# A planned decoder step on one Trainium2 core: eight complex powers move from GpSimd to VectorE, two TensorE steps get a later planned start, and the planner learns of a shared port

## The chip, the cores and the metric

The kernel runs on one core of one Trainium2 chip. The metric is the time of one execution on the device in microseconds (us). The engines are named as in the profile: PE is TensorE (PEld its weight loads), DVE is VectorE, ACT is ScalarE, POOL is GpSimd, and SP (SyncE) issues every DMA.

## The reference

One layer of a hybrid decoder over 2048 prompt tokens and 8 single sample tokens, model width 1024, everything in float32:

```python
h = rmsnorm(x, norm_mix_g)
z = h @ w_in                        # q, k, v | conv a, g | ssm u
attn_out = attend(q, k, v, sinks)   # 8 heads, window 128, ALiBi, sinks
conv_out = conv_module(...)         # GLU, depthwise conv of 31 taps, layer norm, silu
ssm_out  = ssm_module(...)          # 16 groups, 64 complex states, gelu, GLU
x = x + concat(attn_out, conv_out, ssm_out) @ w_out
hf = rmsnorm(x, norm_ffn_g)
x = x + (silu(hf @ w_ff_gate) * (hf @ w_ff_up)) @ w_ff_down
```

A final rmsnorm and the new caches and states are also outputs. Each sample token has a cache of 30 convolution rows, so its convolution needs `cache_conv` beside the new row. In the ssm the matrix that takes 8 tokens at once into a state holds the product of the input matrix with the powers 0 to 7 of each state's complex multiplier.

## The kernel before

**Tiling.** The tokens are cut in four quarters q of 512 columns (the last has 520, with the 8 sample tokens) for everything up to the output projection, and in three groups of 688 and 684 columns for the feed-forward part. A matrix product is made of three float32r products per term (high by high, high by low, low by high), so each weight unit of 128 output rows (a tile `whl`) takes 24 matmuls per column tile. Such a unit is prepared once: SP loads `wraw`, ACT writes the high part, POOL writes the low part (a subtraction, `yield low` in `load_unit`, line 349), and the result is also stored to memory, from where later quarters load it again.

**The first phase** (to about 600 us) runs the projections in the order of line 1280: convolution and ssm inputs of quarter 0, attention inputs of quarter 1, then of quarter 0, and so on to the convolution inputs of quarter 3 (`3c`). Beside it DVE sets up the ssm tables in `setup_ssm` (line 750): a chain of some 200 small instructions, which ends with the discretized input matrix `bb`; then `power(t)` (line 890) makes for each of 8 powers six instructions of 128x128 (four products, a difference, a sum) into the tiles `wr` and `wi`. PE transposes `wr` and `wi` once all eight are done (`yield pw_ev`, line 910). `setup_toeplitz` (line 931) makes, from the same `bb`, nine further steps of six DVE instructions into `GT`, which PE needs too. The convolution (`conv`, line 593) is 60 DVE instructions per quarter on a tile `acc`, followed by `layer_norm_gate` (line 609), which goes from POOL to PE to DVE to ACT and back. `conv_tail` (line 654) does the convolution of the sample tokens: it loads `cache_conv` into `crow`, transposes it on PE, and ends in another `layer_norm_gate` of 8 columns.

**The second phase** (to about 800 us) is the output projection, `out_stream` (line 1624), which adds the residual on DVE, squares on ACT, and sums the squares over the 8 output units on POOL into `ssq`; after the last unit (line 1668) PE multiplies `ssq` by the tile `ones_c`, ACT takes the root and DVE the reciprocal. **The rest** is the feed-forward part.

**What sets the order.** Every engine runs its instructions in the order in which they were issued, and that order is found by a planner while the program is built: class `Flow`. Each piece of work is a generator which yields the engine, the buffers and the events that it needs next. `Flow.run` keeps one planned clock per engine, takes the piece that can start earliest (by priority among those within a small slack), and lets it issue its instructions. `Engine.cost` gives each instruction a planned duration, and `Flow.spent` (line 139) moves the clock of its engine on by that. `Flow.freer` (line 132) picks the engine whose planned clock is behind, with 500 ns in favour of POOL; `power` uses it to choose between POOL and DVE. An `Ev` is an event with a planned time, before which a piece that yields it isn't planned. In the planner of before no engine's clock knows of another's port:

```python
start = max(self.clock[eng], c["begin"] if c["last"] in (None, eng) else c["fin"])
self.clock[eng] = start + ns
```

The planned times only set the order. What an instruction waits for when it runs are the semaphores of the data that it reads and of the buffers that it writes.

Of the kernel before, what the change touches and what calls it, by code (L numbers as in the profile page):

```python
# [13 lines left out]
OP = mybir.AluOpType  # L14
PSUM = bass.MemoryType.PSUM
# [12 lines left out]
NEG = -1.0e30  # L28
W = [512, 512, 512, 520]
TILES = [[(0, 512)]] * 3 + [[(0, 256), (256, 264)]]  # L30
C1 = 6.28125
C2 = 0.0019350051879882812
C3 = 3.0199159819567e-07
# [17 lines left out]
class Flow:  # L51
# [9 lines left out]
    def __init__(self, nc):  # L61
        self.nc = nc
        self.clock = dict.fromkeys(("PE", "ACT", "DVE", "POOL", "SP", "DMA"), 0.0)
        self.free = {}
        self.tasks = []
        self.cur = None
        self.serial = 0
        self.extra = {}

    def buffers(self, **tags):  # L70
        for tag, n in tags.items():
# [57 lines left out]
    def now(self):  # L129
        return self.cur["fin"]  # L130

    def freer(self, *engines):
        return min(engines, key=lambda x: self.clock[x] + self.BIAS.get(x, 0.0))

# [1 line left out]
        self.free[tag].append(self.cur["fin"])  # L136
        self.free[tag].sort()

    def spent(self, eng, ns):
        c = self.cur  # L140
        if c is None:
            return
        ns += self.extra.get(eng, 0.0)
        start = max(self.clock[eng], c["begin"] if c["last"] in (None, eng) else c["fin"])
        self.clock[eng] = start + ns
        c["fin"], c["last"] = max(c["fin"], start + ns + self.LATENCY[eng]), eng
        c["end"], c["prev"] = start + ns, eng
# [15 lines left out]
class Engine:  # L163
# [36 lines left out]
    def __getattr__(self, op):  # L200
        call = getattr(self.engine, op)

        def planned(*args, **kw):
            out = args[0] if args else kw["out"]
            ins = [x for x in args[1:] if isinstance(x, bass.AP)]
            ins += [x for k, x in kw.items() if isinstance(x, bass.AP) and k not in ("out", "accum_out")]
            self.flow.spent(self.name, self.cost(op, out, ins, args, kw))
            return call(*args, **kw)  # L208
        return planned

# [2 lines left out]
def hybrid_step(  # L213
# [10 lines left out]
    fl = Flow(nc)  # L224
# [63 lines left out]
    def stg():  # L288
        return stage.tile([P, 520], F32, tag="stg", name="stg", bufs=N_ST)
# [364 lines left out]
    def conv_tail():  # L654

        yield "SP", "stg", "stg", small_ev, cu_ev[3, 0], cu_ev[3, 1], halo_ev[3]
        cu = CU[3]
        crow = stg()
        for a in range(2):
            dma(crow[:120, a * 256:(a + 1) * 256], cache_conv[0, 4 * a:4 * a + 4].rearrange("b t c -> (b t) c"))  # L660
        cs = stg()[:, 0:2 * NS * TAPS].rearrange("p (i b t) -> p i b t", i=2, b=NS)
        for i in range(2):
            yield "PE", "tr"
            pt = ps_tr()
            for a in range(2):
                E.transpose(pt[:, a * 120:a * 120 + 120], crow[:120, a * 256 + i * P:a * 256 + (i + 1) * P],
                            ident[:120, :120])
            yield "DVE"
            V.tensor_copy(cs[:, i, :, 0:30], pt[:, 0:240].rearrange("p (b t) -> p b t", t=30))
            V.tensor_copy(cs[:, i, :, 30], cu[:, i, 542:550])  # L670
            rel("tr")
        yield "PE", "tr"
        po = ps_tr()
        for i in range(2):
            E.transpose(po[:38, i * P:(i + 1) * P], cu[:, i, 512:550], ident)
        yield "DVE"
        V.tensor_copy(crow[:38, 0:256], po[:38, 0:256])
        rel("tr")
        cu_done(3)
        yield "SP"  # L680
        dma(o_convp[0, 0], crow[:30, 0:256])
        dma(o_convs[0, :, 29, :], crow[30:38, 0:256])
        rel("stg")
        yield "DVE"
        acc = cpool.tile([P, 2, NS], F32, name="acc_s")
        for i in range(2):
            V.tensor_tensor(cs[:, i], cs[:, i], taps[:, i:i + 1, :].to_broadcast([P, NS, TAPS]), op=OP.mult)
            V.tensor_reduce(out=acc[:, i, 0:NS], in_=cs[:, i], op=OP.add, axis=mybir.AxisListType.X)
            V.tensor_scalar(acc[:, i, 0:NS], acc[:, i, 0:NS], fv[:, i:i + 1], None, op0=OP.add)
        rel("stg")  # L690
        fl.add(layer_norm_gate(acc, NS, 3, 512), 2.5)
# [58 lines left out]
    def setup_ssm():  # L750
# [124 lines left out]
        ta, tb = tv(0, 8, 16), tv(1, 8, 16)  # L875
# [12 lines left out]
        pw_ev = Ev(8)  # L888

        def power(t):  # L890
            eng = fl.freer("POOL", "DVE")
            yield eng
            X = G if eng == "POOL" else V
            ta, tb = [tp[:, (2 * (t % 2) + i) * P:(2 * (t % 2) + i + 1) * P].rearrange("p (s c) -> p s c", c=16)
                      for i in range(2)]
            pr, pi = bc16(PW[:, 0, 7 - t, :]), bc16(PW[:, 1, 7 - t, :])
            dr, di = [w.rearrange("p (s t c) -> p s t c", t=8, c=16)[:, :, t, :] for w in (wr, wi)]
            X.tensor_tensor(dr, bb3[0], pr, op=OP.mult)
            X.tensor_tensor(ta, bb3[1], pi, op=OP.mult)
            X.tensor_tensor(di, bb3[0], pi, op=OP.mult)  # L900
            yield eng
            X.tensor_tensor(tb, bb3[1], pr, op=OP.mult)
            X.tensor_tensor(dr, dr, ta, op=OP.subtract)
            X.tensor_tensor(di, di, tb, op=OP.add)
            pw_ev.hit(fl.now())
            if t < 6:
                fl.add(power(t + 2), -900)
# [716 lines left out]
    def out_stream():  # L1624
        for q in range(4):
            yield "stg", Mev[q]
            ssq = stg()
            chain = Ev()
            chain.hit(0.0)
            boxes = []  # L1630
            for m in range(KT):
                ev, box = Ev(), []
                boxes.append((ev, box))
            fl.add(residual(q, 0, *boxes[0]), -600)
            for m in range(KT):
                if m + 1 < KT:
                    fl.add(residual(q, m + 1, *boxes[m + 1]), -400)
                st = {"n": nt[q], "chain": chain}
                chain = Ev()

                def evac(ps, c0, n, q=q, m=m, ev=boxes[m][0], box=boxes[m][1], st=st, ssq=ssq, nxt=chain):
                    yield "DVE", ev
                    x2 = box[0]
                    V.tensor_tensor(x2[:, c0:c0 + n], ps[:, :n], x2[:, c0:c0 + n], op=OP.add)
                    rel("mm")
                    st["n"] -= 1
                    if st["n"]:
                        return
                    yield "SP"
                    dma(x2_d[m][:, 512 * q:512 * q + W[q]], x2[:, :W[q]])  # L1650
                    x2_ev[q, m].hit(fl.now())
                    w = W[q]
                    if m == 0:
                        yield "ACT", st["chain"]
                        S.activation(ssq[:, :w], x2[:, :w], AF.Square)
                        rel("x2")
                        segB_ev.hit(fl.now())
                    else:
                        yield "ACT", "stg"
                        sq = stg()  # L1660
                        S.activation(sq[:, :w], x2[:, :w], AF.Square)
                        rel("x2")
                        segB_ev.hit(fl.now())
                        yield "POOL", st["chain"]
                        G.tensor_tensor(ssq[:, :w], ssq[:, :w], sq[:, :w], op=OP.add)
                        rel("stg")
                    nxt.hit(fl.now())
                    if m == KT - 1:
                        yield "stg"
                        rs = stg()  # L1670
                        for c0, n in TILES[q]:
                            yield "PE", "tr"
                            pm = ps_tr()
                            E.matmul(pm[:, :n], ones_c, ssq[:, c0:c0 + n], start=True, stop=True)
                            yield "ACT"
                            S.activation(rs[:, c0:c0 + n], pm[:, :n], AF.Sqrt, scale=256.0 / D, bias=eps)
                            rel("tr")
                        rel("stg")
                        yield "DVE"
                        V.reciprocal(rs[:, :w], rs[:, :w])  # L1680
                        yield "SP"
                        dma(rs_d[:, 512 * q:512 * q + w], rs[:, :w])
                        rel("stg")
                        rs_ev[q].hit(fl.now())
                yield from dense(outs[KT * q + m], M[q], TILES[q], evac, -500)
            rel("h")

# [366 lines left out]
    b = "B22"  # L2054
# [180 lines left out]
```

## Time and profile before

| | us |
|---|---|
| three runs | 2240.51, 2243.15, 2245.12 (median 2243.15) |
| the profiled execution, its own time | 2244.29 |
| its span, from the first to the last instruction | 2242.5 |

So 1.8 us of the profiled execution's time lie outside its span, and it is 1.1 us above the median. The profile's page gives the busy time of each engine and the chain that ended last. Its timelines list an engine's instructions in order of time, neighbours of one kind merged, with the idle time ahead in brackets and whose result ended it. All matrix work has the line L208 (the planner's helper), so instructions are told apart by the tiles that they write and read: `mm` and `sc` are accumulators of products, `tr` the accumulators for transposes and small products, `s` the tiles of the ssm and of attention, `PW` the powers.

### The profile page before, as it was taken

What the parts mean: (1) busy time and instruction counts of PE and PEld (TensorE: products, weight loads), DVE (VectorE), ACT (ScalarE), POOL (GpSimd) and SP (SyncE); (2) the same over time, 40 slices, a digit from 0 to 9 for tenths busy, and PEclk for the clock granted to TensorE, in tenths of its full rate; (3) what the DMA queues carried; (4) which work ended last, traced back from release to release, by engine and by line L of the source; (5) the groups of instructions that cost most, each with busy time, mean ns of one, the idle gap of its engine ahead of it and who ended that gap; (6) DMA issues with size and microseconds to landing.
All of it is one profiled execution on the core that took longest, in us unless ns stands there. A gap on an engine that the chain in (4) does not pass through costs nothing. (4 is left out here: it accounts for less than half of the span.)

```text
span 2242.5 us, 35196 instructions
## 1 busy us (share of the span) xinstructions
PE 2110.6 (94%) x13326; PEld 1961.5 (87%) x13326; DVE 1554.2 (69%) x3039; ACT 834.9 (37%) x1653; POOL 281.1 (13%) x219
## 2 busy tenths in 40 slices
PE   8779998999889989999999999999999999999997
PEld 8557776777667878999999999999999999999997
DVE  5986988786595567878877765656556755555555
ACT  7116534776333143323323452322223532222223
POOL 3421011002212232222222100000000000000000
PEclk9889999999989999999999999999999999999999
DMA  8856566566769996555664766575665774553651
GB/s 275 250 185 217 180 201 195 157 190 197 250 220 312 332 305 211 199 166 196 196 210 158 250 228 220 181 228 158 190 215 170 235 255 140 180 184 126 191 162 51
DMA packets 350713, 457.90 MB, mean 204 GB/s; under 512 B 42453, under 2 KB 233760, under 8 KB 340304
## 3 DMA queue, kind: packets, MB, share of 16 engines
q1 hardware_dynamic: 350544, 455.66, 63.7%
q8 instruction: 105, 1.72, 0.3%
q14 instruction: 64, 0.52, 0.1%
HBM read 333.94 MB, written 122.32 MB: 203 GB/s over the span
## 5 line engine op out<-in xcount | busy, mean ns | idle before, releaser
L208 PE MATMUL mm<-h,whl 128*128 128x342 f32 (+4 forms) x7296 | 1277.3, 331 | 37.7 <-POOL whl L208 13.9
L208 PEld LDWEIGHTS mm<-h,whl 128*128 128x128 f32 x7296 | 1156.4, 191 | 106.1 <-issue 20.4
L208 PE MATMUL sc<-act,whx 128*128 128x342 f32 (+1 forms) x3168 | 517.6, 321 | 8.3 <-DVE xa L208 6.4
L208 PEld LDWEIGHTS sc<-act,whx 128*128 128x128 f32 x3168 | 501.3, 189 | 12.5 <-DVE xa L208 10.6
L208 DVE TENSOR_TENSOR xa<-xa,sc 128x342 f32<-128x342 f32 (+1 forms) x528 | 266.0, 510 | 235.5 <-PE sc L208 226.6
L208 DVE SCALAR_TENSOR_TENSOR acc<-cu,taps,acc 128x512 f32<-128x512 f32 x240 | 174.6, 791 | 0.1
L208 POOL TENSOR_TENSOR whl<-sw,whl 128x512 fp32r<-128x512 f32 x88 | 124.6, 1427 | 344.6 <-ACT whl L208 337.5
L208 ACT ACTIVATE whx<-wraw 128x1024 fp32r<-128x1024 f32 x66 | 66.6, 1053 | 240.3 <-PE sc L208 238.8
L208 ACT ACTIVATE stg<-mm 128x342 f32<-128x342 f32 (+3 forms) x100 | 49.5, 499 | 252.0 <-PE mm L208 249.8
L208 PE MATMUL mm<-hb,whl 128*128 128x342 f32 (+1 forms) x792 | 135.8, 320 | 0.0
L208 PEld LDWEIGHTS mm<-hb,whl 128*128 128x128 f32 x792 | 126.5, 189 | 0.4 <-ACT gs L208 0.4
L208 ACT ACTIVATE whl<-wraw 128x512 fp32r<-128x512 f32 (+1 forms) x122 | 84.7, 696 | 68.5 <-PE mm L208 28.2
L208 DVE TENSOR_TENSOR stg<-mm,stg 128x342 f32<-128x342 f32 (+1 forms) x132 | 67.7, 513 | 57.2 <-PE mm L208 55.0
L208 ACT ACTIVATE act<-gs 128x342 fp32r<-128x342 f32 (+1 forms) x99 | 48.3, 488 | 145.4 <-DVE gs L208 145.4
L208 DVE TENSOR_TENSOR whl<-wraw,whl 128x512 fp32r<-128x512 f32 x102 | 78.1, 766 | 30.9 <-ACT whl L208 28.7
L208 ACT ACTIVATE s<-s,sst 128x256 f32<-128x256 f32 (+1 forms) x180 | 83.4, 486 | 10.9 <-DVE sst L208 10.8
L208 ACT ACT_TABLE_LOAD x58 | 74.4, 1283 | 30.4 <-DVE acc L208 10.9
L208 DVE TENSOR_TENSOR whl<-xraw,whl 128x512 fp32r<-128x512 f32 x96 | 76.5, 802 | 11.1 <-ACT whl L208 11.1
L208 DVE TENSOR_TENSOR whx<-wraw,whx 128x1024 fp32r<-128x1024 f32 x66 | 79.0, 1236 | 5.5 <-ACT whx L208 2.2
L208 ACT ACTIVATE whl<-sw 128x512 fp32r<-128x512 f32 x88 | 53.1, 625 | 75.9 <-PE mm L208 28.2
L208 ACT ACTIVATE whl<-xraw 128x512 fp32r<-128x512 f32 x96 | 60.0, 625 | 49.0 <-issue 29.7
L208 DVE TENSOR_TENSOR gs<-mm,gs 128x342 f32<-128x342 f32 (+1 forms) x66 | 33.7, 511 | 59.9 <-PE mm L208 59.9
(233 smaller groups left out, 1890.6 us busy)
## 6 DMA issues: line engine op xcount, KB each, us to landing
whl<-sum SPq DMA_DIRECT2D x176, 512.0 KB
sum<-whl SPq DMA_DIRECT2D x88, 512.0 KB
wraw<-in_w_ff_down SPq DMA_DIRECT2D x66, 512.0 KB
whl<-hl_o SPq DMA_DIRECT2D x24, 1024.0 KB
wraw<-in_w_ff_up SPq DMA_DIRECT2D x44, 512.0 KB
xraw<-in_w_ff_gate SPq DMA_DIRECT2D x42, 512.0 KB
whl<-hl_q SPq DMA_DIRECT2D x12, 1024.0 KB
tx<-hraw SPq DMA_DIRECT2D x14, 684.0 KB
```

The costliest lines, as they stand in the source:

```text
L208: return call(*args, **kw)
```

## The change

It has four edits. `power` no longer asks which engine is behind: all of its instructions go to DVE. `conv_tail` adds an event 6 us after its load of `cache_conv`, so that the planner puts the transposes of `crow` no earlier. In `out_stream` the product with `ones_c` gets an event 8 us after the last sum of squares. And the planner keeps a list of the times at which POOL, and DVE instructions with two operands of more than one column outside PSUM, hold a port in common: an instruction of the one isn't planned to start inside a time of the other.

```diff
+RS_LATE = 8000.0
...
+    def later(self, ns):
+        ev = Ev()
+        ev.hit(self.cur["fin"] + ns)
+        return ev
...
-    def spent(self, eng, ns):
+    def spent(self, eng, ns, port=False):
...
         start = max(self.clock[eng], c["begin"] if c["last"] in (None, eng) else c["fin"])
+        if port:
+
+            for a, b in self.port["POOL" if eng == "DVE" else "DVE"]:
+                if a <= start < b:
+                    start = b
+            self.port[eng] = self.port[eng][-40:] + [(start, start + ns)]
         self.clock[eng] = start + ns
...
-            self.flow.spent(self.name, self.cost(op, out, ins, args, kw))
+            both = self.name == "DVE" and sum(x.space != PSUM and x.free_size() > 1 for x in ins) > 1
+            self.flow.spent(self.name, self.cost(op, out, ins, args, kw), self.name == "POOL" or both)
...
         cs = stg()[:, 0:2 * NS * TAPS].rearrange("p (i b t) -> p i b t", i=2, b=NS)
+        ready = fl.later(6000.0)
         for i in range(2):
-            yield "PE", "tr"
+            yield "PE", "tr", ready
...
         def power(t):
-            eng = fl.freer("POOL", "DVE")
-            yield eng
-            X = G if eng == "POOL" else V
+            yield "DVE"
...
-            X.tensor_tensor(dr, bb3[0], pr, op=OP.mult)
+            V.tensor_tensor(dr, bb3[0], pr, op=OP.mult)
...
                     if m == KT - 1:
-                        yield "stg"
+                        yield "stg", fl.later(RS_LATE)
```

The order of all engines moves with the planned times, from about 20 us on. From the middle of the first group of the feed-forward part to the end the kinds of the instructions follow each other as before on PE, DVE and ACT. Three places show what moved. The numbers behind a name tell tiles of one kind apart and differ between the kernels.

On POOL, at the end of the preparation of the first 12 weight units (`whl<-wraw,whl`), before. Here `s2_1085` holds `bb`, `s4_1103` and `s4_1104` are `wr` and `wi`, and `s2_1105` is the tile for temporary products:

```order
L208 TENSOR_TENSOR whl_1026<-wraw_918,whl_1026 128x1024
L208 TENSOR_TENSOR s4_1103<-s2_1085,PW_168 128x8x16
L208 TENSOR_TENSOR s2_1105<-s2_1085,PW_168 128x128
L208 TENSOR_TENSOR s4_1104<-s2_1085,PW_168 128x8x16
L208 TENSOR_TENSOR whl_1093<-wraw_998,whl_1093 128x1024
L208 TENSOR_TENSOR s2_1105<-s2_1085,PW_168 128x128
```

And now (`whl_1046` is the unit that was `whl_1093`, `whl_1139` the one that was `whl_1199`):

```order
L222 TENSOR_TENSOR whl_972<-wraw_845,whl_972 128x1024
L222 TENSOR_TENSOR whl_1046<-wraw_963,whl_1046 128x1024
L222 TENSOR_TENSOR whl_1139<-wraw_1019,whl_1139 128x1024
L222 MEMSET TT_173 128x2048
```

The subtraction of the eleventh unit stood behind the first three instructions of a power and stands now right behind the tenth unit; the 36 instructions of six powers have left the engine. All 48 stand on DVE one behind the other, between the sum that ends `bb` (and two taps of the convolution) and the nine steps into `GT`, with which two of the powers had been interleaved.

On PE, the eleventh and twelfth unit and the transposes of the powers, before:

```order
L208 MATMUL mm_1120<-h_212,whl_1026 128x512 x24
L208 MATMUL mm_1213<-h_212,whl_1093 128x512 x24
L208 MATMUL mm_1284<-h_212,whl_1199 128x512 x24
L208 MATMUL tr_1341<-ident_96,s4_1103 128x128 x4
L208 MATMUL tr_1352<-GT_172,s2_1085 16x128 x16
L208 MATMUL tr_1375<-ident_96,s4_1103 128x128 x4
L208 MATMUL mm_1382<-h_205,whl_1201 128x512 x6
```

And now (`s4_1218` is `wr`, `s2_489` the output matrix of the ssm; the first product with `GT` stands 54 matmuls of 512 columns behind `tr_1317`):

```order
L222 MATMUL mm_1114<-h_212,whl_1046 128x512 x24
L222 MATMUL mm_1182<-h_212,whl_1139 128x512 x18
L222 MATMUL tr_1221<-ident_96,s2_489 128x128 x4
L222 MATMUL mm_1182<-h_212,whl_1139 128x512 x6
L222 MATMUL mm_1271<-h_205,whl_1141 128x512 x18
L222 MATMUL tr_1317<-ident_96,s4_1218 128x128 x4
L222 MATMUL mm_1271<-h_205,whl_1141 128x512 x6
```

Eighteen matmuls of a unit of quarter 0 have come ahead of the first transposes of the powers, and the products with `GT` have gone behind them. Also, the two transposes with which the ssm's set-up begins stand three column tiles (72 matmuls of 256 columns) and 8 transposes of inputs later than before.

On PE, the sample tokens' convolution and the statistics of quarter 0, before (`stg_6191` is `crow`, `stg_4511` is `ssq`, `stg_6285` holds the 8 columns, `ss` is a tile of the sample tokens' attention, `h_6040` the input of the output projection of quarter 1):

```order
L208 MATMUL tr_6201<-s_5938,Z_6130 64x128 x8
L208 MATMUL tr_6224<-ident_96,stg_6191 128x120 x2
L208 MATMUL tr_6241<-ident_96,stg_6191 128x120 x2
L208 MATMUL tr_6248<-stg_4511,ones_c_105 128x512
L208 MATMUL tr_6255<-ident_96,cu3_1808 38x128 x2
L208 MATMUL tr_6262<-ident_96,ss_6211 128x64
L208 MATMUL tr_6288<-stg_6285,ones_c_105 128x8
L208 MATMUL mm_6298<-h_6040,whl_5991 128x512 x6
```

And now (`stg_4837` is `crow`, `h_3584` the input of the output projection of quarter 0, `kk`, `qq` and `s` are tiles of attention):

```order
L222 MATMUL mm_4933<-h_3584,whl_4365 128x512 x6
L222 MATMUL sc_4944<-ident_96,s_4703 128x128 x4
L222 MATMUL tr_4951<-ident_96,stg_4837 128x120 x2
L222 MATMUL sc_4958<-ident_96,s_4703 128x128 x4
L222 MATMUL sc_4966<-kk_3614,qq_4588 128x256 x4
L222 MATMUL mm_4933<-h_3584,whl_4365 128x512 x12
L222 MATMUL tr_5006<-ident_96,xo_4905 128x128 x4
```

The sample tokens' convolution has moved from behind all attention into the first unit of the output projection of quarter 0, with attention blocks around it; the `ones_c` products follow one by one between blocks (that of quarter 0's `ssq` in the second unit of quarter 1). Most of the projections `3c` stood behind the eighth unit of the output projection of quarter 0 and now all of them stand ahead of its first. Attention ended inside that quarter's fifth unit; now it runs on beside the projection of quarter 1, to its sixth unit.

## Rows read from the trace of the kernel before

**Rows 1.** The page, busy time and share of the span

```profile
PE 2110.6 (94%) x13326; PEld 1961.5 (87%) x13326; DVE 1554.2 (69%) x3039; ACT 834.9 (37%) x1653; POOL 281.1 (13%) x219
```

**Rows 2.** Busy time by stretch; last three columns granted clock, DMA share, GB/s

```profile
50.00:135.00 85.00, 57.88 (x310) 46.14 (x308) 81.98 (x262) 16.03 (x25) 45.15 (x45) 0.78 0.78 236
330.00:600.00 270.00, 250.22 (x1634) 197.75 (x1634) 197.68 (x637) 161.15 (x456) 35.87 (x21) 0.96 0.65 191
330.00:680.00 350.00, 308.53 (x1914) 243.94 (x1914) 273.25 (x778) 185.07 (x500) 50.63 (x33) 0.93 0.66 202
350.00:400.00 50.00, 45.85 (x331) 37.61 (x330) 43.61 (x105) 28.87 (x69) 5.84 (x4) 0.93 0.58 166
600.00:640.00 40.00, 21.70 (x117) 17.25 (x117) 38.06 (x91) 15.28 (x29) 6.53 (x7) 0.70 0.52 175
```

**Rows 3.** Timeline of PE, 30 to 152 us; in brackets the idle time before

```profile
37.80 3.08 PE L208 MATMUL mm<-h,whl 128*128 128x256 f32 x24
...
97.12 8.61 PE L208 MATMUL mm<-h,whl 128*128 128x512 f32 x24 [13.59 <-POOL whl L208]
...
124.27 1.11 PE L208 MATMUL tr<-ident,s 128*128 128x128 f32 x4 [12.87 <-POOL s L208]
...
137.25 14.19 PE L208 MATMUL mm<-h,whl 128*128 128x512 f32 x60
```

**Rows 4.** Timeline of POOL, 90 to 120 us

```profile
91.85 2.46 POOL L208 TENSOR_TENSOR s<-s,PW 128x128 f32<-128x128 f32 x3 [16.42 <-DVE s L208]
94.28 2.79 POOL L208 TENSOR_TENSOR whl<-wraw,whl 128x1024 fp32r<-128x1024 f32 x1
...
111.73 7.11 POOL L208 TENSOR_TENSOR s<-s,PW 128x128 f32<-128x128 f32 x3 [1.64 <-DVE s L208]
```

**Rows 5.** Timeline of ACT, 75 to 90 us

```profile
78.17 1.06 ACT L208 ACTIVATE whl<-wraw 128x1024 fp32r<-128x1024 f32 x1 [4.76 <-DMA wraw<-in_w_in]
...
87.78 1.06 ACT L208 ACTIVATE whl<-wraw 128x1024 fp32r<-128x1024 f32 x1 [3.94 <-DMA wraw<-in_w_in]
```

**Rows 6.** Timeline of DVE, 48 to 140 us

```profile
49.93 0.29 DVE L208 COPY glw<-s 128x256 f32<-128x256 f32 x1 [0.54 <-DMA s<-in_ssm_glu_w]
50.61 2.02 DVE L208 COPY glw<-s 128x256 f32<-128x256 f32 x1 [0.39 <-DMA s<-in_ssm_glu_w]
...
60.75 2.29 DVE L208 TENSOR_TENSOR PW<-s 128x8 f32<-128x8 f32 x1
...
91.17 0.61 DVE L208 TENSOR_TENSOR s<-s 128x128 f32<-128x128 f32 x2
...
99.31 1.83 DVE L208 TENSOR_TENSOR s<-s,PW 128x128 f32<-128x128 f32 x4
...
110.57 0.88 DVE L208 TENSOR_TENSOR s<-s,PW 128x128 f32<-128x128 f32 x4
111.38 0.48 DVE L208 TENSOR_TENSOR s<-s,s 128x128 f32<-128x128 f32 x2
111.78 0.89 DVE L208 TENSOR_TENSOR s<-s,PW 128x128 f32<-128x128 f32 x4
...
124.13 16.18 DVE L208 SCALAR_TENSOR_TENSOR acc<-cu,taps,acc 128x512 f32<-128x512 f32 x24
```

**Rows 7.** Timeline of PE, 604 to 632 us

```profile
611.63 1.03 PE L208 MATMUL tr<-ident,stg 120*128 120x120 f32 x4 [5.61 <-DMA stg<-in_cache_conv]
616.13 2.08 PE L208 MATMUL tr<-stg,ones_c 128*128 128x512 f32 x2 [3.47 <-POOL stg L208]
...
628.22 0.59 PE L208 MATMUL tr<-stg,ones_c 128*128 128x8 f32 x2 [8.03 <-POOL stg L208]
628.67 2.91 PE L208 MATMUL mm<-h,whl 128*128 128x512 f32 x6
```

**Rows 8.** Timeline of PE, the statistics of the last quarter

```profile
812.29 1.14 PE L208 MATMUL tr<-stg,ones_c 128*128 128x256 f32 x4 [1.51 <-POOL stg L208]
```

More of the change, by code (lines that the diff above doesn't have):

```diff
@@ L68, in __init__ @@
         self.extra = {}
+        self.port = {"DVE": [], "POOL": []}
     def buffers(self, **tags):
@@ L897, in power @@
             dr, di = [w.rearrange("p (s t c) -> p s t c", t=8, c=16)[:, :, t, :] for w in (wr, wi)]
-            X.tensor_tensor(dr, bb3[0], pr, op=OP.mult)
[L899 to L904, printed above, removed]
+            V.tensor_tensor(dr, bb3[0], pr, op=OP.mult)
+            V.tensor_tensor(ta, bb3[1], pi, op=OP.mult)
+            V.tensor_tensor(di, bb3[0], pi, op=OP.mult)
+            yield "DVE"
+            V.tensor_tensor(tb, bb3[1], pr, op=OP.mult)
+            V.tensor_tensor(dr, dr, ta, op=OP.subtract)
+            V.tensor_tensor(di, di, tb, op=OP.add)
             pw_ev.hit(fl.now())
```

## The prediction

> **What bounds the kernel now.** I read the page's busy shares first, then windows by stretch, then the timelines of PE and of those it waited for. PE is busy for 2110.6 us of a span of 2242.5 [rows 1], so 131.9 us of idle time is all that any order could give back, apart from the clock. From the middle of the feed-forward part's first group on, the kinds of instructions follow each other as before, so I look for the effect ahead of it, in two stretches. From 50 to 135 us PE is busy for 57.88 of 85 us, at a mean granted clock of 0.78 of full speed; from 600 to 640 us it is 21.70 of 40, at 0.70 [rows 2]. [...] DVE is nearly full in both (81.98 of 85, 38.06 of 40).
>
> In the first stretch PE stands still twice: 13.59 us for a weight tile from POOL and 12.87 us for the powers [rows 3]. In the timelines of POOL and ACT the reader is to see that the weight tile had no need to be late. ACT had its high part at 78.17 + 1.06 = 79.2 us [rows 5], but POOL's subtraction began at 94.28, because the three instructions ahead of it on POOL belong to a power and had waited 16.42 us for DVE's `bb` [rows 4], which ended at 91.8 [rows 6]. The second stop is the slow making of the powers themselves. In the second stretch PE waits in order for `cache_conv` (5.61), for the statistics of quarter 0 (3.47) and for the sample tokens' layer norm (8.03) [rows 7].
>
> **Powers on DVE, and the weight tile freed.** POOL loses 36 instructions and DVE gains them; on each engine nothing else is added or removed, and no DMA.
>
> PE's arrival first. PE stopped at 97.12 - 13.59 = 83.5 us. The eleventh unit's subtraction can now follow at 79.2 and takes some 2.5 us (2.79 in [rows 4]), so at 81.7 it is ahead of PE and the 13.59 us go. One matmul of 512 columns takes 14.19 / 60 = 0.237 us [rows 3], a unit of 24 takes 5.7: PE is done at 89.2. What is late next is the twelfth unit: its data let ACT begin at 87.78 [rows 5], so with 1.06 and 2.5 us it is there at 91.3. PE waits 2.1 us, does the unit and 18 more matmuls (10.0 us, and 0.6 for four transposes), and stands at the powers at 101.9. On SP, the store of the eleventh unit and the loads behind it no longer wait for POOL either; should the unit of the 18 matmuls still land late, that wait lies inside the one for the powers.
>
> Now the powers. `bb` was done at 91.8 [rows 6]. Three things delay it. (a) The set-up's first transposes stand behind 72 more matmuls, 3 x 3.08 us [rows 3], and 8 transposes, some 10 us. The chain had slack there: it stood until the load of `glw` had landed, at 50.6 [rows 6]. I estimate that 2.5 us of the 10 come through; the bounds are 0 and 10.2. (b) Three scaled evictions have come ahead of `bb`, about as long as a tap (16.18 / 24 = 0.67 us [rows 6]): 2.0 us. (c) The two last subtractions on POOL now fall into the chain. An instruction on 8 columns took 2.29 us in it once [rows 6], while POOL subtracted, so each costs at most some 2.1: I take one of the two. That gives 91.8 + 2.5 + 2.0 + 2.1 = 98.4. Two taps follow (1.4), then 48 instructions. A power alone on DVE goes from 110.57 to 111.78, 1.21 us [rows 6]; eight take 9.7. PE gets them at 109.7, after a wait of 7.8 us. Before it got them at 124.27, with 18 matmuls (4.3 us) less done: 124.27 + 4.3 - 109.7 = 18.9 us are gained. With all of (a) and both of (c) the gain is 9; with neither it is 23. The low clock after the stop stays (the 24 matmuls after 13.59 us of idle took 8.61 instead of 5.7 us [rows 3]). The steps into `GT`, now behind the powers, take nine times 1.21 us or 11 us, up to about 122; PE asks for them 54 matmuls (13 us) and four transposes later, at about 125, so they hide; if not, 2 or 3 us come back. I take **-18**, of 9 to 23.
>
> The trace says why this is no matter of DVE's rate. With POOL at the powers too, four of DVE's products took 1.83 us, and 0.88 without it [rows 6]; three of POOL's took 7.11 us while DVE was at work and 2.46 elsewhere [rows 4]. So the engines took turns, and two at work were no faster than one. [...]
>
> Can PE keep 18 us that DVE doesn't gain? Between 330 and 600 us DVE was busy for 197.68 of 270 us [rows 2], so it has 72 us of slack there.
>
> **The new order from 330 us on.** [...] By the order, conv tail, taps and late attention now share the time with the output projection, so the 18.3 us of idle time at 600 to 640 have no reason to stay in one place: the transposes of `crow` and the sums have attention and weight units ahead of them. What remains is the ordinary loss beside attention. From 330 to 600 us that was 19.8 of 270 us idle and a clock of 0.96, together some 10% [rows 2]; 296.5 / 0.9 = 329, a gain of 21. In the densest attention, 350 to 400 us, it was 4.15 of 50 idle at 0.93, together some 13% [rows 2]; 296.5 / 0.87 = 341, a gain of 9. DVE's 273.25 us must fit: in 329 us it is 83% busy, near the 87% of that densest stretch and above the 73% of the 270 us. I take between them, **-13**. The bounds: -21, and where DVE can't run denser than 73%, 273.25 / 0.73 = 374 us, a loss of 24.
>
> **The shared port in the planner** adds no instruction. The statistics' later event costs nothing where other units fill PE, and in the last quarter saves at most its wait of 1.51 us [rows 8]: **-1**. What the planner still leaves out shows in one row: a copy with a single operand took 2.02 us where its twin took 0.29 [rows 6], so DVE is also held up in instructions that the edit doesn't count. [...] If two such stops of 1.7 us fall into the chain ahead of `bb`, the first term is -15 and the sum 3 us higher.
>
> **The sum** is 2244.3 - 18 - 13 - 1 = 2212 for an execution such as the profiled one; the median of the runs is 1.1 us lower, so I forecast 2211.
>
> **The rivals.**
> - Only the powers pay: the waits of 600 to 640 us come back in small pieces around attention, since DVE is as full there. 2244 - 18 - 1 - 1 = 2224. For it: DVE's 95% in that stretch. Against: the taps can be put anywhere.
> - More than forecast: the chain isn't delayed and attention runs at the ordinary loss. -23 and -21: 2198.
> - No gain: the 18 us are lost again before 600 us because DVE paces PE, and the second stretch keeps its waits. 2243. For it: DVE's 81.98 of 85 us in the first stretch [rows 2], which its new work lengthens. Against: the 72 us of slack behind.
> - Slower: DVE becomes the bound where attention now runs beside the output projection, in that it gets no denser than the 73% it had beside attention. +24 there; with -18 and -1 it gives 2248, and up to 2266 if that stretch also swallows the first gain. It decides as soon as the loss there passes 24 us. For it: 83% is needed, and POOL's weight subtractions and sums of squares hold up DVE there too. Against: 87% was reached for 50 us.
>
> **How the numbers follow.** Forecast 0.51 (2203 to 2219), only the powers 0.18, more 0.16, no gain 0.06, slower 0.09. A measurement tells 0.2% or 4.5 us from no change, so faster means under 2238.7: 0.85; same 0.06; slower, over 2247.6, 0.09. The range, 2195 to 2240, takes in the first three and the bounds of the terms, and leaves out most of the last two.
>
> **What would show it.** Right: no wait of PE for a weight tile near 84 us; powers on DVE in one run of about 10 us; a wait of PE for DVE of some 8 us ahead of the transposes; no idle stretch over 4 us between 560 and 680 us; feed-forward matmuls beginning about 30 us earlier. Wrong: a wait for the powers of 15 us or more, PE's idle time beside attention over 13%, or a new wait behind 800 us.

## The result, and the profile of the changed kernel

The changed kernel takes 2188.57 us, the median of 4 runs (2182.84 to 2191.76), beside 2241.83 for the kernel before in the same session: a ratio of 0.976, with a 95% interval of 0.9738 to 0.9783. It is 53 us faster, where 32 were forecast, and lies below the range. The profiled execution took 2186.88 us, its span 2185.1.

The page's busy times ([rows 1] shows before):

```profile
PE 2091.2 (96%) x13326; PEld 1950.1 (89%) x13326; DVE 1533.9 (70%) x3052; ACT 853.7 (39%) x1682; POOL 254.0 (12%) x183
```

PE's idle time fell from 131.9 to 2185.1 - 2091.2 = 93.9 us, and its busy time by 19.4 us though its work is the same; the mean granted clock of the span is 0.987, and was 0.974. The stretches of [rows 2]:

```profile
50.00:135.00 85.00, 70.45 (x385) 57.36 (x384) 78.80 (x293) 20.86 (x32) 16.13 (x7) 0.94 0.90 274
330.00:600.00 270.00, 257.69 (x1711) 206.85 (x1710) 246.12 (x710) 182.00 (x488) 45.25 (x28) 0.99 0.75 229
330.00:680.00 350.00, 336.27 (x2078) 267.77 (x2077) 290.03 (x781) 215.47 (x553) 64.52 (x43) 1.00 0.78 246
350.00:400.00 50.00, 46.78 (x342) 40.16 (x342) 48.37 (x140) 31.20 (x96) 4.51 (x2) 1.00 0.78 249
600.00:640.00 40.00, 40.00 (x192) 30.02 (x191) 23.52 (x47) 20.91 (x45) 10.92 (x9) 1.00 0.80 257
```

The reader is to see three things. From 330 to 680 us PE is idle for 13.7 us, not 41.5, and its granted clock is 1.00, not 0.93. From 350 to 400 us DVE is busy for 48.37 of 50 us and PE loses nothing by it. And the stretch from 600 to 640 us, which lost almost half of PE's time, is full.

PE around the powers ([rows 3] shows before), in its timeline:

```profile
89.23 0.73 PE L222 MATMUL mm<-h,whl 128*128 128x512 f32 x2 [0.38 <-ACT whl L222]
91.66 3.99 PE L222 MATMUL mm<-h,whl 128*128 128x512 f32 x16 [1.69 <-POOL whl L222]
99.31 4.45 PE L222 MATMUL mm<-h,whl 128*128 128x512 f32 x18 [1.83 <-DVE stg L222]
114.41 1.11 PE L222 MATMUL tr<-ident,s 128*128 128x128 f32 x4 [10.65 <-DVE s L222]
```

and DVE at the end of `bb`, and the first and the last instructions of the eight powers ([rows 6]):

```profile
102.91 0.62 DVE L222 TENSOR_TENSOR s<-s 128x128 f32<-128x128 f32 x2
...
104.77 0.89 DVE L222 TENSOR_TENSOR s<-s,PW 128x128 f32<-128x128 f32 x4
105.57 0.49 DVE L222 TENSOR_TENSOR s<-s,s 128x128 f32<-128x128 f32 x2
...
114.04 0.51 DVE L222 TENSOR_TENSOR s<-s,s 128x128 f32<-128x128 f32 x2
```

The 13.59 us for the weight tile are gone, and PE waits once, 10.65 us, for the powers.

**Where the time came from.** To compare the two traces at equal progress I add up PE's work along its timeline, each matmul at the duration that its kind has at a granted clock of 1.00 (one of 512 columns 0.237 us), and read at which time each trace has done the same amount. By how much the change is then ahead (its lead, us):

| PE work done, us | 80 | 100 | 140 | 240 | 300 | 400 | 520 | 560 | 620 | 760 |
|---|---|---|---|---|---|---|---|---|---|---|
| lead | 25.5 | 17.9 | 13.8 | 12.3 | 15.8 | 31.7 | 30.3 | 46.9 | 51.0 | 55.7 |

With other averages for the kinds these leads move by some 3 us, and by more where one of the two traces stands still, so only larger differences are read from them. There are three pieces: 14 to 18 us at the powers, of which 12 are left by 240; some 16 to 20 between 300 and 400 of work, in the densest attention; and some 20 where the old stops of [rows 7] were. What moved behind the last two shows in when DVE begins the instructions that write `cu`, the convolution inputs (first and last start), before and now, between 380 and 700 us (the four of the last quarter, whose 60 taps need them):

```profile
L208 DVE TENSOR_TENSOR cu<-mm,stg x4: 419/423/426, 511.1 to 606.9; 128x256 f32<-128x256 f32 x2, 128x264 f32<-128x264 f32 x2
```

```profile
L222 DVE TENSOR_TENSOR cu<-mm,stg x4: 424/426/433, 426.0 to 454.2; 128x256 f32<-128x256 f32 x2, 128x264 f32<-128x264 f32 x2
```

The projection `3c` ends 153 us earlier, so the last quarter's taps lie beside attention and output projection, not behind them.

### The profile page after: what moved, and what is told of

It reads as the page before. It is cut to its first block, busy times and chain, and to the rows that moved or that the text cites. A ratio compares the mean times of both kernels' runs of the same rounds, so it can differ in the third digit from the quotient of the medians.

```text
span 2185.1 us, 35164 instructions
## 1 busy us (share of the span) xinstructions
PE 2091.2 (96%) x13326; PEld 1950.1 (89%) x13326; DVE 1533.9 (70%) x3052; ACT 853.7 (39%) x1682; POOL 254.0 (12%) x183
## 4 chain that ended last, share of the span: by engine, by line
PE 54%; DMA 3%; DVE 2%; issue 1%; ACT 1%; POOL 1%; SPq 0%; DVEq 0%; ACTq 0%; POOLq 0%
PE mm L222 34%; PE sc L222 20%; DMA tx<-hraw 1%; DMA xa<-x 1%; DVE sw L222 1%; POOL whl L222 1%; PE tr L222 1%; ACT whl L222 0%; DMA whl<-sum 0%; ACT h L222 0%; DVE h L222 0%; DVE act L222 0%; DVE gs L222 0%; DVE xa L222 0%; DVE stg L222 0%
## 5 line engine op out<-in xcount | busy, mean ns | idle before, releaser
L222 ACT ACTIVATE s<-s,sst 128x256 f32<-128x256 f32 (+1 forms) x196 | 90.3, 488 | 13.3 <-DVE sst L222 13.3
```

## Experiments

The theory as forecast: the powers on DVE give some 18 us, the two later events the rest, the port in the planner nothing. "The port" is here the planner's list of busy times; of POOL and DVE side by side the traces show durations, and these stand where they were read. Rival A: the port in the planner makes the gain. Rival B: no edit has a price of its own; each new order falls out as it falls. All runs below are medians of several executions beside runs of the kernel before on the same chip; the ratio is to those.

### One edit at a time

Powers on DVE alone (of the change's diff only `power` with `yield "DVE"` and `V.`):

> The kernel before with one edit of the four: all eight powers on DVE. Theory as predicted: the gain of 18 us at the powers stays to the end, 2220 to 2228 us. Rival A (the port in the planner makes the rest): the same here, 2220 to 2228, but the lead shrinks to some 12 us by 320 us, as it does in the trace of the change. Rival B (no edit has a price of its own, each new order falls out as it falls): anywhere from 2200 to 2245, and the stops of 5.6, 3.5 and 8.0 us at 604 to 632 us may stay or go.

The port alone (`power` with `fl.freer` again, no events):

> The kernel before with one edit of the four: the planner counts the shared port; the powers are still given to the engine that is planned to be free first. Theory as predicted: the port adds nothing, 2236 to 2248 us, the weight tile behind the powers on POOL still late near 84 us. Rival A: the port puts the order beside attention right (PE's granted clock 1.00 from 330 to 600 us, idle there under 14 us of 270), 2205 to 2225. Rival B: 2200 to 2245, with no relation to what the other kernels show.

The two events alone:

> The kernel before with the two later events alone (6 us behind the load of the sample tokens' convolution rows, 8 us behind the last sum of squares). Theory as predicted: the stops of 5.6 and 3.5 us at 604 to 632 us go, perhaps the one of 8.0 too, nothing before changes: 2222 to 2234 us. Rival A: only the stop for the rows and that for the statistics go, part of it comes back elsewhere: 2232 to 2242. Rival B: 2200 to 2245.

And the change without the port:

```diff
-self.name == "POOL" or both)
+False)
```

> The changed kernel without the port in the planner (powers on DVE and the two later events stay). Theory as predicted (the port is worth nothing, the later events carry the second stretch): 2183 to 2194 us, as the change. Rival A (the port carries the second stretch): 2210 to 2226, with the clock from 330 to 600 us back under 0.98. Rival B: 2185 to 2230.

| | us | ratio, 95% interval |
|---|---|---|
| powers alone | 2246.8 | 1.0018 (1.0005 to 1.0031) |
| port alone | 2204.2 | 0.9841 (0.9815 to 0.9867) |
| events alone | 2247.1 | 1.0030 (1.0019 to 1.0041) |
| all but the port | 2229.7 | 0.9948 (0.9929 to 0.9966) |

The forecast's theory falls: its -18 alone gives nothing, and its zero gives 37 us. All but the port gives 11. Powers and events alone lie above every range given for them, and the port alone (just below A's) and all but the port only in Rival B's. Rival A's second sign failed too: with the port alone PE is idle for 21.7 us of the 270 from 330 to 600 us, at a clock of 0.95, so beside attention that order is no fuller than before (19.8 at 0.96).

PE with the powers alone:

```profile
78.77 8.61 PE L222 MATMUL mm<-h,whl 128*128 128x512 f32 x36
109.65 1.12 PE L222 MATMUL tr<-ident,s 128*128 128x128 f32 x4 [22.27 <-DVE s L222]
```

The wait for the weight tile is gone here too, as reasoned from the order on POOL. But PE arrives at the transposes at 87.4 us, 16 us earlier than in the change, and stands there for 22.27 us. Summed along PE's timeline, 396 projection matmuls stand ahead of these transposes here, 432 before and 450 in the change. So the powers come 14.6 us earlier than before (109.65 instead of 124.27), with 36 matmuls (8.5 us at 0.237) less done; 6 us are gained. The lead is 6.4 us at 80 us of work and 1.8 at 240. The port alone puts 486 matmuls ahead: with it the planner takes the powers for later.

```profile
119.35 1.09 PE L222 MATMUL tr<-ident,s 128*128 128x128 f32 x4 [6.22 <-DVE s L222]
```

There the powers come 4.9 us earlier than before with 54 matmuls (12.8 us) more done, a gain of 17.7, though half of them still run on POOL. The same count gives 9.9 + 4.3 = 14.1 us for the change.

### What the edits add beside the port

The change with `power` and `fl.freer` as before:

> The changed kernel with the powers given again to the engine that is planned to be free first (port and two later events stay). If the powers on DVE are worth what the forecast gave them once the planner counts the port: 2200 to 2212 us, 12 to 18 over the change. If the port alone carries the first stretch (the port alone had a lead of 21 us at the powers, the powers alone 9): within 8 us of the change, 2181 to 2197, the lead behind the powers again 13 us or more.

The change without its two events:

> The changed kernel without the two later events (powers on DVE, port in the planner). The port alone gave 2204 and the change 2189; the 15 us between are the powers' or the later events'. If they are the later events': 2200 to 2208, with waits of PE for the sample tokens' rows or for the statistics of 3 us or more again. If they are the powers': 2185 to 2193.

| | us | ratio, 95% interval |
|---|---|---|
| port and events | 2209.2 | 0.9848 (0.9834 to 0.9863) |
| port and powers | 2188.1 | 0.9750 (0.9736 to 0.9765) |

The events add nothing: 2188.1 without them, 2188.6 with. The powers seem to add 16 to 21 us, and both times lie in the ranges that say so. But not at the powers: without them the lead is larger there (17.1 at 140 us of work, some 20 at 300), a few us smaller from 400 on, and far smaller only from about 540; `3c` ends at 559.9 us and not at 454.2.

So I ran the powers at another place in the same order. Four of the eight are planned as on DVE, and run on POOL behind the twelfth unit's subtraction:

```diff
+            def tt(out, x, y, op):
+                if t % 2 == 0:
+                    fl.spent("DVE", V.cost("tensor_tensor", out, [x, y], (), {}), True)
+                    return G.engine.tensor_tensor(out, x, y, op=op)
+                return V.tensor_tensor(out, x, y, op=op)
```

> The changed kernel, planned as it is, order of every engine as in the change, but four of the eight powers (the even ones, 24 instructions) run on POOL, behind the twelfth weight unit's subtraction, so that no weight tile stands behind them. If where the powers run has a price of its own (two engines take turns at the port): PE gets the powers 3 to 8 us later, 2191 to 2198 us. If it was only the queue and the order that counted: PE gets them within 1 us of 114.4, or earlier, 2184 to 2191.

Measured: 2191.3 us, a ratio of 0.9782 (0.9743 to 0.9821), which holds the change's 0.976. POOL, DVE and PE, in this order:

```profile
102.67 2.47 POOL L915 TENSOR_TENSOR s<-s,PW 128x128 f32<-128x128 f32 x4 [10.59 <-DVE s L222]
105.11 0.95 POOL L915 TENSOR_TENSOR s<-s,s 128x128 f32<-128x128 f32 x2
106.02 1.67 POOL L915 TENSOR_TENSOR s<-s,PW 128x128 f32<-128x128 f32 x4
...
103.99 1.76 DVE L222 TENSOR_TENSOR s<-s,PW 128x128 f32<-128x128 f32 x4
105.67 0.94 DVE L222 TENSOR_TENSOR s<-s,s 128x128 f32<-128x128 f32 x2
106.54 1.76 DVE L222 TENSOR_TENSOR s<-s,PW 128x128 f32<-128x128 f32 x4
...
114.00 1.09 PE L222 MATMUL tr<-ident,s 128*128 128x128 f32 x4 [9.59 <-DVE s L222]
```

From one power to the next DVE takes 106.54 - 103.99 = 2.55 us, and POOL does another meanwhile; DVE alone does two in 2.42 (four of its products take 1.76 us here and 0.89 in the change). PE gets the powers at 114.0 and in the change at 114.4, as the second range says, though the time lies at the edge of the first. `bb` ended 0.9 us earlier here (102.6, not 103.5), so the shared powers were some 0.5 us slower. Where they ran had no larger price in this order, in which no weight tile stands behind them.

### Which half of the port, or any delay

Only DVE stands back, POOL is planned as before:

```diff
-            for a, b in self.port["POOL" if eng == "DVE" else "DVE"]:
+            for a, b in self.port["POOL"] if eng == "DVE" else []:
```

> The changed kernel, but in the planner only DVE stands back for POOL; POOL isn't held up by DVE. Theory (the gain is that DVE's planned time comes out later, so that PE's projections are planned ahead of steps that depend on DVE): 2183 to 2198 us, clock 0.98 or more from 330 to 600 us. Rival (both engines' planned times count, POOL's weight tiles above all): 2205 to 2225.

No port; DVE's instructions are planned 8% longer:

```diff
-        return 67.0 + 61.0 * cols + per * n + dep
+        return 1.08 * (67.0 + 61.0 * cols + per * n + dep)
```

> The changed kernel without the port; in its place the planner takes every DVE instruction for 8% longer, about the time that the port added to DVE's planned clock up to 600 us (39 us). If any later planned DVE does it: 2185 to 2205 us. If it must be the port, since only it puts the delay where POOL works: 2218 to 2235, as without the port.

Measured: 2193.6 (0.9777, 0.9763 to 0.9792) and 2204.2 (0.9823, 0.9807 to 0.9840). Both lie in the first of their two ranges, the second at its end. DVE's half of the port does nearly all of it, and a plain 8% does 26 of the 41 us that the port is worth there. It need not be the port.

### The place of the last quarter's projection

The list of projections, in the kernel before and then in the change:

```diff
-"0c 0u 1k 0k 1u 1c 2c 2u 3u 2k 3k 3c"
+"0c 0u 1k 0k 1u 1c 2c 2u 3u 2k 3c 3k"
```

> The kernel before with one word moved in the list of projections: the convolution inputs of the last quarter ahead of its attention inputs, not behind. None of the four edits. Theory (the largest piece of the gain, from 330 to 640 us, is that these inputs come some 150 us earlier, so that the 60 taps of the last quarter lie beside attention and not behind it): the taps start by 520 us, the stops of 3.5 and 8.0 us at 616 to 632 us go, 2208 to 2228 us. Rival (the gain is that DVE's and POOL's planned times fit better everywhere; where the inputs stand is a by-product): 2234 to 2250.

> The changed kernel with the same word moved. Its inputs of the last quarter are already done by 454 us, so by the theory little is left to gain: 2180 to 2196 us. Rival (still earlier is better, since DVE has room from 135 to 330 us): 2165 to 2180.

Measured: 2244.1 (1.0009, 0.9990 to 1.0027) and 2207.2 (0.9847, 0.9815 to 0.9879). The first lies in the rival's range, the second in neither. The theory falls in this form. In the kernel before, `3c` ends at 404.7 us and the taps at 525.7, the lead is 13.2 us at 400 us of work, and then it is lost again in new stops of PE, at other steps:

```profile
583.35 2.08 PE L208 MATMUL tr<-stg,ones_c 128*128 128x512 f32 x2 [5.08 <-POOL stg L208]
593.22 0.59 PE L208 MATMUL tr<-ident,kvT 128*8 128x128 f32 x2 [7.79 <-DMA kvT<-kT]
...
600.31 1.94 PE L208 MATMUL tr<-ident,s 128*128 128x128 f32 x8 [3.65 <-ACT h L208]
```

My reading is that, moved by hand, one block of DVE's work has changed places with another, and that what pays is steps which wait for DVE standing next to matmuls that don't, up to the end. No run tests this by itself.

### Counting more at the port

The planner counts DVE's copies and scalar operations at the port too:

```diff
-... for x in ins) > 1
+... for x in ins) > (op not in ("tensor_copy", "tensor_scalar"))
```

> The changed kernel, with DVE's copies and scalar operations between SBUF tiles counted at the port too (a copy took 2.02 us beside POOL where its twin took 0.29). If the plan gets better with every instruction that is really held up: 2175 to 2187 us. If the count only matters as time added to DVE's clock, and that is enough already: 2184 to 2200.

Measured: 2193.5 us (0.9785, 0.9750 to 0.9820), no better than the change and in the second range. The copy of [rows 6] took 2.02 us and its twin 0.29; it ended 0.16 us behind a subtraction of POOL (49.98 to 52.47 us). But a planner that counts such copies finds no faster order.

### How far apart orders lie, and DVE planned longer

Three kernels with a nudge, `"DVE": 160.0` for `140.0` in `LATENCY`: the kernel before, the port alone, and the change.

> The kernel before, with the planner's delay behind a DVE instruction taken as 160 ns, not 140: a small nudge to the order and nothing else. It tells how far times lie apart that differ by the order alone. If the order before is a typical one for its planner: 2232 to 2254 us. If the time falls out as the order falls: it may be as low as 2215 or as high as 2270.

> The kernel before with the port in the planner alone, and the same nudge of 20 ns. The port alone gave 2204, the port with powers on DVE 2188. If the 16 us between belong to the powers: 2199 to 2209 us. If they are the luck of one order behind 540 us (the powers have no price of their own, as their place in the fixed order showed): as often as not below 2197.

> The changed kernel with the same nudge of 20 ns. If the change's time belongs to its edits: 2184 to 2194 us. If its stretch behind 540 us is luck: 2194 to 2210, while the lead at 500 us stays at 25 us or more.

The kernel before with nothing but 8% and then 16% in the formula for DVE, and the change with 8%:

> The kernel before, where the planner takes every DVE instruction for 8% longer; none of the four edits, no port. If a later planned DVE carries the gain, with or without the powers: 2195 to 2220 us, the lead at 300 us 10 us or more. If it needs the powers beside it: 2235 to 2250.

> The kernel before, where the planner takes every DVE instruction for 16% longer; none of the four edits. With 8% it took 2196.5 us. If what counts is that DVE's planned times are no shorter than the measured ones, 16% gives no more than 8%: 2188 to 2206 us. If every later planned DVE is better: 2165 to 2186. If planning too long costs as much as too short: 2215 or more.

> The changed kernel, port and all, where the planner also takes every DVE instruction for 8% longer. If port and longer DVE do the same thing, the second adds nothing: 2184 to 2204 us, inside what orders alone differ by. If they correct different things and add up: 2160 to 2180.

| | us | ratio, 95% interval | `3c` ends | lead at 560 |
|---|---|---|---|---|
| before, nudged | 2228.9 | 0.9939 (0.9915 to 0.9963) | 598.5 | 5.2 |
| port alone, nudged | 2198.3 | 0.9803 (0.9782 to 0.9824) | 460.8 | 36.9 |
| change, nudged | 2198.2 | 0.9800 (0.9778 to 0.9823) | 446.6 | 29.1 |
| before, DVE 8% longer | 2196.5 | 0.9794 (0.9774 to 0.9814) | 462.7 | 34.6 |
| before, DVE 16% longer | 2209.6 | 0.9846 (0.9824 to 0.9867) | 570.7 | 25.1 |
| change, DVE 8% longer | 2173.3 | 0.9689 (0.9674 to 0.9704) | 445.0 | 49.1 |

A nudge that means nothing moves the kernel before by -13 us, the port alone by -6 and the change by +10. The first lies in its second range, the next between its two. So less than some 15 us between two of these kernels says nothing about an edit. Rival B holds inside that, and not beyond: the six orders with the whole port as the change counts it (2188.1 to 2209.2) and the five with neither port nor longer DVE, in the unchanged list of projections (2228.9 to 2247.1), don't overlap. With the nudge, the port with the powers and without them take the same. The nudged change is in its second range, but it loses ground ahead of the place that this supposes: from 330 to 600 us PE is busy for 249.58 us at a clock of 0.96, not 257.69 at 0.99. So beside attention three of the six orders with the port (247.7 to 249.6 us busy) are no fuller than the kernel before (250.2). What all six share, and all four with longer DVE, is the stretch from 600 to 640 us: PE is busy for 39.2 to 40.0 of its 40 us there, and for 19.9 to 28.0 in the five with neither.

The kernel before with DVE planned 8% longer, without any of the four edits, is as fast:

```profile
330.00:680.00 350.00, 335.12 (x2052) 265.14 (x2052) 303.36 (x812) 210.88 (x539) 59.27 (x40) 0.98 0.78 241
```

Its powers run partly on POOL, and its weight tile isn't late; PE's next stop there is 9.16 us for DVE, then 10.21 for the powers. With 16% it is slower than with 8%, and in none of its ranges: later is not simply better. The change with 8% on top is the fastest kernel of the study, 2173.3 us. Its lead over the change is 15 us, as much as a nudge can move; that the two corrections add up is not shown.

One rival had no run of its own. Four places of the kernel give a scaling or a copy to whichever of ACT and DVE is planned to be free first (`fl.freer("ACT", "DVE")`), so a later planned DVE also hands work to ACT. By the traces DVE has 141 of these instructions in the kernel before, 118 in the change, 133 with the port alone, 129 in the kernel before with 8%, and 84 in the change with 8%. It can't be the main cause: the port alone moves 8 and gains 37 us, and the kernel before with the moved list also has 133 and gains nothing. In the fastest kernel it may have a part.

## Why the prediction was wrong

**The term that failed in size: "the new order from 330 us on", taken as -13, with -21 as its lower bound.** From 300 to 760 us of PE work the lead grew by 55.7 - 15.8 = 40 us. The step was to divide the work of 296.5 us by 0.9 or 0.87, "the ordinary loss beside attention" of 10 to 13%. No run shows the 296.5 us, which were my estimate. What the traces show of the stretch from 330 to 680 us is 41.5 us idle and a granted clock of 0.50 for 47.8 us before (it was 1.00 for the rest), and in the change 13.7 us idle, 4%, and 0.50 for 3.4 us. The loss that I took for a property of attention was one of the old order, in which PE came to a step before DVE had done the one ahead of it: between 330 and 600 us PE waited 18.6 of its 19.8 idle us for DVE and ACT.

```profile
PE sc L208 <- DVE s L208: 9.6, 9, 2.8
PE sc L208 <- DVE mx L208: 5.3, 4, 2.2
PE sc L208 <- ACT s L208: 3.3, 1, 3.3
PE tr L208 <- DVE s L208: 0.4, 1, 0.4
```

Each line gives who waited for whom, the us in total, the number of waits and the longest. In the change the three `sc` lines have 3.0, 0.2 and 0.3 us. I also bounded DVE by the density that it had reached, 73 and 87%; it ran at 91% for 270 us and 97% for 50. DVE's idle time there was mostly waiting for PE (47.4 of 72.3 us from 330 to 600, 18.6 for `sc` alone), not a limit.

**The term that failed in its cause: -18 for the powers on DVE.** The size at that place is somewhat too large: counted as the forecast counts it, 14.1 us are gone, not 18.9, and PE waits 10.65 us for the powers where 7.8 were forecast. Its pieces: `bb` ended at 103.5 us, not 98.4, PE arrived at 103.8, not 101.9, and the powers took 9.7 us, as forecast. The chain ahead of `bb` was under-sized in (a), since the second copy of `glw` began 4.7 us later (55.29, not 50.61), and in (c), since beside each of the two last subtractions and a MEMSET behind them an instruction of the chain was long (2.41, 2.39 and 1.64 us where others of their shapes take 0.2 to 0.3). But the runs give the gain to the order that the port makes: 6 us with the move alone, 17.7 with the port alone. I took what the order of the change showed (18 matmuls ahead of the transposes) as part of the edit to `power`, and never asked which edit had put them there. Of the move alone 1.8 us of lead are left at 240 us of work and nothing at the end, and with the order held fixed the place of the powers had no price. With the move alone (2246.8 beside 2240.8 us) the weight tile was no longer late, and PE waited for the powers in its place. Two slips are in that working: the pieces of 109.7 add up to 109.5, and where three of POOL's products took 2.46 us DVE was at work too, on taps (91.69 to 94.86 us).

**"The shared port in the planner adds no instruction", at nothing.** True of the instructions, and the reason why it was left out of the sum; it is the edit that sets the order everywhere, and alone it gives 37 us. Nor is it true that on each engine nothing is added or removed but the powers: 23 scalings and copies have gone from DVE to ACT.

**"Can PE keep 18 us that DVE doesn't gain?"** Not all: of 14.1 us by the count, or 17.9 by the lead at 100 us of work, 12.3 were left at 240. I named 72 us of slack from 330 us on, and the loss fell ahead of it. From 100 to 240 us of work the change took 140 us (130 to 270), the kernel before 135 (148 to 283), nearly the same stretch of work: PE was idle for 6.5 us instead of 4.0 and busy for 133.47 instead of 131.01, at a clock of 0.99 instead of 1.00, while DVE was busy for 117.87 us instead of 112.19, the same share (84 and 83%). What caused the loss wasn't tried by itself.

**Of the signs:** right were no long wait for the weight tile near 84 us, the powers in one run of 9.7 us, and no idle time over 4 us between 560 and 680 us. Of the signs of being wrong, the first two did not come, and behind 800 us PE has only short new waits (the longest, 2.7 us, for `tx`). The feed-forward matmuls begin 48 us earlier (751.16, not 799.22), not 30. Behind their start there are small waits:

```profile
751.16 0.42 PE L222 MATMUL mm<-h,whl 128*128 128x344 f32 x1 [3.20 <-ACT h L222]
...
764.42 0.66 PE L222 MATMUL mm<-h,whl 128*128 128x344 f32 x1 [3.87 <-ACT h L222]
...
787.20 9.37 PE L222 MATMUL mm<-h,whl 128*128 128x344 f32 x48 [3.58 <-DVE gs L222]
```

The kernel before has as many there (3.17, 2.85 and 3.40 us at 799, 816 and 860 us), and they cost no lead (53.2 at 700 us of work, 55.7 at 760). Of the rivals, "more than forecast" had the right sign of the error, for the wrong reason: the chain ahead of `bb` was delayed.

**What stays open.** Why 8% is enough: whether DVE's planned times are then true on the average, or steps behind DVE merely get a margin. That 16% gives less speaks against a margin alone, but by 13 us, as much as orders differ anyway. Also why some orders with the port keep PE fuller beside attention and others don't. And whether the powers on DVE are worth something beside the port: three orders with them took 2188.1 to 2198.2 us, three without 2198.3 to 2209.2.

## What to carry to other kernels

Where a planner sets the order, an edit to its costs moves every instruction and may be the largest edit of all, though it adds none: ask of each piece of the new order which edit put it there, and run the edits one at a time. Before a difference between two orders is given a cause, nudge the plan by something that means nothing and see how far the time moves; here it was 6 to 13 us. And a loss that one order shows beside some work is no price of that work: check who waits for whom before it is used as a bound.

## What the runs showed of the hardware that was not expected

DVE and PE were both nearly full at once in the changed kernel: 48.37 and 46.78 of 50 us, at a granted clock of 1.00, in the densest attention (350 to 400 us).

Beside POOL some taps of the convolution were longer, and others not. In the change a run of taps ends with these ten, and a short copy and ten more follow:

```profile
349.81 6.71 DVE L222 SCALAR_TENSOR_TENSOR acc<-cu,taps,acc 128x512 f32<-128x512 f32 x10
...
356.77 8.45 DVE L222 SCALAR_TENSOR_TENSOR acc<-cu,taps,acc 128x512 f32<-128x512 f32 x10
```

The second ten took 1.7 us more. Only their first two were longer, 1.45 and 1.78 us; the other eight took 0.74 each, as the ten before them did. POOL had two instructions at work from 354.86 to 359.37 us. The last two of the first ten taps, begun at 355.11 and 355.77 us, ran beside them at 0.74 all the same, and the second long tap ended 0.55 us behind them:

```profile
354.86 4.51 POOL L222 TENSOR_TENSOR stg<-s,s 128x512 f32<-128x512 f32 x2 [31.86 <-ACT s L222]
```
